# A hybrid decoder layer: nudged half chunks of weights run low x high first, one more half chunk is nudged, and the last query transposes move half a chunk later

## The chip, the cores and the metric

The kernel runs on one core of one Trainium2 chip. The metric is the device time of one execution in microseconds (us); lower is better. The engines are TensorE (PE; its weight loads are PEld), VectorE (DVE), ScalarE (ACT), GpSimd (POOL) and SyncE (SP), which issues most DMAs.

## The reference

One layer for 256 tokens of width 2048, in fp32: an RMS norm, one wide input projection, two token mixers side by side (sparse attention "NSA", and a gated DeltaNet), gated and summed, an output projection, and a gated feed-forward network (FFN) of width 5632.

```python
h = rms_norm(x, norm1_w)
proj = h @ w_in
nsa_q, nsa_kv, nsa_g, dn_qkv, dn_z, dn_a, dn_b, merge_g = split(proj)
o_nsa = nsa_mixer(rope(nsa_q), nsa_kv, nsa_g, ...)
o_dn = gated_deltanet(dn_qkv, dn_z, dn_a, dn_b, ...)   # conv of 4 taps, SiLU, l2 norms,
                                                       # a triangular solve per chunk, a scan
g_nsa, g_dn = split(sigmoid(merge_g))
x = x + (g_nsa * (o_nsa @ w_up_nsa) + g_dn * (o_dn @ w_up_dn)) @ w_o
h2 = rms_norm(x, norm2_w)
x = x + (silu(h2 @ w_ffn_gate) * (h2 @ w_ffn_up)) @ w_ffn_down
out = rms_norm(x, norm_f_w)
```

## The kernel before

**Three matmuls for one.** Every large matrix product is made of fp32r matmuls. Weights and activations are each split into a high part and a remainder, and high x high, high x low and low x high are summed in PSUM; low x low is left out. Activations are kept in this form (`hh`, `odn`, `onsa`, `h2`). Weights come from HBM in chunks of 1 MB (`raw`, three buffers). Each chunk is split in two half chunks by `split`: ScalarE writes the high part (`hi`, line 161), VectorE the remainder (`lo`, line 162), each into one of three buffers.

**group_t**, the function that the change is mostly about, makes two transposed output tiles of 128 features by 256 tokens. The weights are the stationary operand, the activations move. One call takes one or two chunks of 8 blocks of 128 rows, and a half chunk is 24 matmuls on line 238 of 128x256: 16 with the weights `hi` (8 by the activation's high part, 8 by its low part), then 8 with `lo`. In the trace a half chunk is a row `mm<-hh,hi` x16 and a row `mm<-hh,lo` x8; in the text these are the high run and the low run. From about 55 us on, group_t makes the DeltaNet inputs, the NSA inputs, the merge gates, both up projections (`odn`, `onsa`) and the FFN's gate and up products (`h`), which are 88 chunks.

**Work between the half chunks.** After each half chunk `pump` moves one step on in each of three lanes of Python generators; what they emit lands at that place of TensorE's order. `prep_k`, `prep_v`, `prep_q` are run for two groups of four heads each: they convolve (`conv_taps`, line 403 on VectorE, a SiLU on line 407 of ScalarE), transpose on TensorE in plain fp32 (`ktr`, `vtr`, `qtr`), and make products of 128x128 (`G`, `A`). `solve` does the triangular solve on VectorE (lines 497 and 499) and begins with one small transpose `bT`. Each `yield` in a generator is a delay of half a chunk. TensorE follows its order strictly; VectorE's and ScalarE's orders come from a scheduler, which puts the splits well ahead.

**The nudge.** After most of the fp32 pieces the generators set `self.nudge = True`. The next half chunk of group_t then writes its `lo` 16 floats (64 bytes) further into its buffer, and the flag is cleared:

```python
hv, lv = self.split(rv, 256, h, 16 * self.nudge)
self.nudge = False
```

Thirteen half chunks are nudged: behind gcT, both ktr, both G, both vtr, both qtr, both A, at the start of the `odn` products, and behind the transposes R of the second norm's factor, at the start of the FFN. The half chunk behind bT is not.

Of the kernel before, what the change touches and what calls it, by code (L numbers as in the profile page):

```python
# [14 lines left out]
P = 128  # L15
# [82 lines left out]
class Kern:  # L98
# [122 lines left out]
    def group_t(self, srcs, acts, out=None):  # L221

        nc = self.nc
        ps = self.pmain.tile([P, 2, 512], F32, tag="mm", name=self.nm("mm"))[:, :, 0:256]
        n = len(srcs)
        for c, src in enumerate(srcs):
            rv = self.load(src, 256, nk=8)
            for h in range(2):  # L230

                hv, lv = self.split(rv, 256, h, 16 * self.nudge)
                self.nudge = False
                for p in range(3):
                    for k in range(4):
                        a = acts(c * 8 + h * 4 + k)
                        for f in range(2):
                            nc.tensor.matmul(ps[:, f], (hv, hv, lv)[p][:, k, f * P:f * P + P], a[:, p % 2, :],  # L238
                                             start=c + h + p + k == 0, stop=c == n - 1 and h + p + k == 6,
                                             skip_group_check=True)  # L240
                self.pump()
        if out is None:
            return ps
        nc.scalar.activation(out, ps, AF.Copy)
        return out
# [211 lines left out]
    def solve(self):  # L457

        nc, V = self.nc, self.nc.vector
        ar = self.ar  # L460
        Lb = ar.alloc([32, 32], "xm")
        Tb = ar.alloc([32, 32], "xm")
        pr = ar.alloc([32, 32], "xm")
        bank = self.aux("bT")
        self.pin(nc.tensor.transpose(bank[:16, :128], self.brk[:].rearrange("p a b -> p (a b)"), self.cs["ident"]))
        bT = self.ar.alloc([128])
        V.tensor_copy(bT[:16, :], bank[:16, :128])
        bb = self.small([32], "bb")
        for blk in range(4):
            self.pin(nc.gpsimd.dma_start(bb[16 * blk:16 * blk + 16, :], bT[:16, 32 * blk:32 * blk + 32]))  # L470
        bT.free()
        scr = self.dram.tile([4, 16, 32, 32], F32, name="scrM")
        scrT = self.dram.tile([64, 32, 32], F32, name="scrT")
        scrTT = self.dram.tile([64, 32, 32], F32, name="scrTT")
        nc.gpsimd.memset(Tb[:64], 0.0)
        nc.gpsimd.memset(Tb[:64].rearrange("p a b -> p (a b)")[:, 0:1024:33], 1.0)
        for b in range(4):
            sl = slice(32 * b, 32 * b + 32)
            nc.gpsimd.dma_start(scr[b].rearrange("h j i -> j h i"), self.MT[sl, :, sl])
        nc.gpsimd.dma_start(Lb[:64], scr[:].rearrange("b h j i -> (b h) j i"))  # L480
        self.D = ar.alloc([16, 128], "wm")
        self.DT = ar.alloc([16, 128], "wm")
        nc.gpsimd.memset(self.D.ap, 0.0)
        nc.gpsimd.memset(self.DT.ap, 0.0)

        for q in range(4):
            self.pin(V.tensor_tensor(self.MT[:, 4 * q:4 * q + 4, :], self.MT[:, 4 * q:4 * q + 4, :],
                                     self.cs["offmask"][:, None, :].to_broadcast([P, 4, 128]), op=OP.mult))
            if q % 2:
                yield  # L490
        self.pin(V.tensor_tensor(Lb[:64], Lb[:64], bb[:64, None, :].to_broadcast([64, 32, 32]), op=OP.mult))
        yield
        prf = pr[:64].rearrange("p a b -> p (a b)")
        for j in range(31):
            n, m = 31 - j, j + 1
            pv = prf[:, :n * m].rearrange("p (a b) -> p a b", b=m)
            self.pin(V.tensor_tensor(pv, Lb[:64, j, j + 1:32].unsqueeze(2).to_broadcast([64, n, m]),  # L497
                                     Tb[:64, j, 0:m].unsqueeze(1).to_broadcast([64, n, m]), op=OP.mult))
            self.pin(V.tensor_tensor(Tb[:64, j + 1:32, 0:m], Tb[:64, j + 1:32, 0:m], pv, op=OP.subtract))
            if j % 2 or 10 < j < 20:  # L500
                yield
        diag = [slice(32 * b, 32 * b + 32) for b in range(4)]
        nc.gpsimd.dma_start(scrT[:], Tb[:64])
        for b, sl in enumerate(diag):
            nc.gpsimd.dma_start(self.D[sl, :, sl], scrT[16 * b:16 * b + 16].rearrange("h i c -> i h c"))
        for _ in range(2):
            yield
        self.pin(nc.scalar.activation(pr[:64], Tb[:64].rearrange("p a b -> p b a"), AF.Copy))
        nc.gpsimd.dma_start(scrTT[:], pr[:64])
        for b, sl in enumerate(diag):  # L510
            nc.gpsimd.dma_start(self.DT[sl, :, sl], scrTT[16 * b:16 * b + 16].rearrange("h c i -> c h i"))
        Lb.free()
        Tb.free()
        pr.free()
        for _ in range(6):
            yield
# [17 lines left out]
    def prep_q(self, pre, cT, hg):  # L534
        nc, V = self.nc, self.nc.vector
        yield from self.conv_taps(pre, cT, hg * 4)
        yield
        self.qT[hg] = cT
        ss = self.small([2, 4], "ssq", bufs=2)
        for t in range(2):  # L540
            bank = self.aux("qtr")
            bv = self.v4(bank)
            for j in range(4):
                nc.tensor.transpose(bv[:, j, :], cT[:, j, t * P:(t + 1) * P], self.cs["ident"])
            sq = self.ar.alloc([4, 128], "zyxm")
            nc.scalar.activation(sq.ap, bv, AF.Square)
            V.tensor_reduce(ss[:, t, :], sq.ap, axis=AX.X, op=OP.add)
            sq.free()
        self.nudge = True
        V.tensor_scalar(ss[:], ss[:], EPS, None, op0=OP.add)  # L550
        rq = self.rsqrt(ss[:], [2, 4], "rq")
        V.tensor_scalar(self.cq[:, :, hg * 4:hg * 4 + 4], rq[:], SCALE, None, op0=OP.mult)
        for _ in range(3):
            yield
        for t in range(2):
            self.nudge = True
            bank = self.aux("A")
            bv = self.v4(bank)
            for j in range(4):
                nc.tensor.matmul(bv[:, j, :], self.kT[hg][:, j, t * P:(t + 1) * P], cT[:, j, t * P:(t + 1) * P], start=True, stop=True)  # L560
            E = self.E[t, hg]
            V.tensor_tensor(E.ap, bv, E.ap, op=OP.mult)
            self.attnT[t, hg] = E
        for _ in range(2):
            yield
# [1031 lines left out]
```

## Time and profile before

| | |
|---|---|
| median of 3 runs | 1456.73 us (1455.71 to 1456.77) |
| the profiled execution | 1456.47 us, of which 1454.7 us are the span from first to last instruction |
| granted TensorE clock, mean | 0.997 |
| busy share of the span | TensorE 99%, VectorE 67%, ScalarE 49%, GpSimd 9% |

A row of a timeline gives start (us from the span's start), busy us, engine, line, operation, out<-in, shape and count; in brackets stands the idle time before it and what ended it. Equal instructions that follow each other are one row. Matmuls overlap, so the busy time of a row reaches into the next one; how long a run keeps TensorE is the difference of the starts of two rows.

### The profile page before, as it was taken

Reading aid. Unit: us, or ns where it says so; the run is one execution under the profiler, and the core shown is the slowest. Engines: PE = TensorE matmul, PEld = TensorE weight load, DVE = VectorE, ACT = ScalarE, POOL = GpSimd, SP = SyncE. Lnnn points to the kernel's source line nnn. Section 1 sums busy time; section 2 is a strip of 40 time slices with the busy share of each in tenths; the row PEclk is TensorE's granted clock in tenths of the full one; section 3 lists DMA queues with packets and bytes.
Section 4 is the critical chain, followed back from the end, with each engine's and each line's share of the span. In section 5 each row is a group of like instructions: output and inputs, shape, how many; then the busy total and the mean of one; then the engine's idle time right before and its main releaser. Section 6 shows DMA issues by size and latency. Waiting matters only on the chain.

```text
span 1454.7 us, 26218 instructions
## 1 busy us (share of the span) xinstructions
PE 1440.7 (99%) x10985; PEld 1377.0 (95%) x10985; DVE 981.5 (67%) x1425; ACT 710.7 (49%) x880; POOL 128.8 (9%) x93
## 2 busy tenths in 40 slices
PE   9999999999999999999999999999999999999996
PEld 9999999999999999998899999999999998888885
DVE  7678997767687755566565555555555558778776
ACT  6655444355455546445454444444434446545554
POOL 1000101000000000120000000000000002313221
PEclk9999999999999999999999999999999999999998
DMA  8664546345554455555555555555555555555653
GB/s 286 230 213 174 181 164 222 121 145 204 201 200 146 146 203 178 194 195 187 179 198 193 188 200 198 183 200 199 184 197 203 184 193 183 195 206 213 210 195 131
DMA packets 48023, 277.12 MB, mean 191 GB/s; under 512 B 5776, under 2 KB 6304, under 8 KB 22048
## 3 DMA queue, kind: packets, MB, share of 16 engines
q1 hardware_dynamic: 44928, 267.98, 52.7%
q10 hardware_dynamic: 1872, 4.82, 0.9%
q0 software_dynamic: 1104, 2.64, 0.6%
q8 instruction: 86, 1.41, 0.4%
q14 instruction: 33, 0.27, 0.1%
HBM read 272.52 MB, written 2.89 MB: 189 GB/s over the span
## 4 chain that ended last, share of the span: by engine, by line
PE 96%; DVE 3%; DMA 0%; issue 0%; ACT 0%; SPq 0%; DVEq 0%; ACTq 0%
PE mm L238 64%; PE mm L1367 5%; PE mm L1365 5%; PE mm L1366 5%; PE mm L265 4%; PE mm L266 3%; PE mm L264 3%; DVE lo L162 1%; PE oacc L931 1%; PE U L601 1%; PE mmx L1367 1%; PE mmx L1365 1%; PE mmx L1366 1%; DMA raw<-in_zab 0%; DVE main L403 0%; DVE xs L497 0%
## 5 line engine op out<-in xcount | busy, mean ns | idle before, releaser
L162 DVE TENSOR_TENSOR lo<-raw,hi 128x1024 fp32r<-128x1024 f32 (+2 forms) x422 | 508.2, 1206 | 297.8 <-ACT hi L161 296.8
L161 ACT ACTIVATE hi<-raw 128x1024 fp32r<-128x1024 f32 (+2 forms) x422 | 440.3, 1046 | 501.9 <-PE mm L238 382.9
L238 PE MATMUL mm<-h,hi 128*128 128x256 f32 x2816 | 348.5, 276 | 0.0
L238 PEld LDWEIGHTS mm<-h,hi 128*128 128x128 f32 x2816 | 332.6, 188 | 0.1
L238 PE MATMUL mm<-hh,hi 128*128 128x256 f32 x2304 | 291.1, 279 | 0.0
L238 PEld LDWEIGHTS mm<-hh,hi 128*128 128x128 f32 x2304 | 275.3, 188 | 0.6 <-ACT hi L161 0.4
L238 PE MATMUL mm<-h,lo 128*128 128x256 f32 x1408 | 188.2, 276 | 0.0
L238 PEld LDWEIGHTS mm<-h,lo 128*128 128x128 f32 x1408 | 172.7, 188 | 0.0
L238 PE MATMUL mm<-hh,lo 128*128 128x256 f32 x1152 | 155.6, 277 | 0.0
L238 PEld LDWEIGHTS mm<-hh,lo 128*128 128x128 f32 x1152 | 142.6, 188 | 0.0
L1354 DVE TENSOR_TENSOR lo<-raw,hi 128x1024 fp32r<-128x1024 f32 (+1 forms) x88 | 122.4, 1402 | 23.9 <-ACT hi L1353 23.0
L1353 ACT ACTIVATE hi<-raw 128x1024 fp32r<-128x1024 f32 (+1 forms) x88 | 88.1, 1001 | 73.0 <-PE mm L1367 47.7
L1260 POOL TENSOR_TENSOR sgt<-sgt,R 128x512 f32<-128x512 f32 x22 | 33.3, 1513 | 530.1 <-ACT sgt L1259 530.1
L265 PE MATMUL mm<-lo,xa 128*128 128x512 f32 x128 | 50.1, 392 | 0.0
L266 PE MATMUL mm<-hi,xa 128*128 128x512 f32 x128 | 50.1, 391 | 0.0
L264 PE MATMUL mm<-hi,xa 128*128 128x512 f32 x128 | 49.8, 389 | 0.0
L1181 POOL TENSOR_TENSOR main<-main 128x512 f32<-128x512 f32 x7 | 15.1, 2163 | 379.2 <-DVE main L1180 379.2
L265 PE MATMUL mm<-lo,hh 128*128 128x354 f32 (+2 forms) x128 | 44.2, 346 | 0.4 <-DVE lo L150 0.3
L264 PE MATMUL mm<-hi,hh 128*128 128x354 f32 (+2 forms) x128 | 43.9, 349 | 0.3 <-ACT hi L148 0.2
L266 PE MATMUL mm<-hi,hh 128*128 128x354 f32 (+2 forms) x128 | 43.7, 341 | 0.0
L1366 PE MATMUL mm<-lo,fa 128*128 128x512 f32 x112 | 43.7, 390 | 0.0
L1353 ACT ACTIVATE hi<-d 128x1024 fp32r<-128x1024 f32 x24 | 25.5, 1061 | 37.3 <-PE mm L1367 20.0
(400 smaller groups left out, 1766.8 us busy)
## 6 DMA issues: line engine op xcount, KB each, us to landing
raw<-in_wfg SPq DMA_DIRECT2D x88, 1024.0 KB, 4.7
raw<-in_wd SPq DMA_DIRECT2D x88, 512.0 KB, 4.2
raw<-in_wmg SPq DMA_DIRECT2D x32, 1024.0 KB, 4.8
raw<-in_wdn SPq DMA_DIRECT2D x24, 1024.0 KB, 4.8
raw<-in_nsa SPq DMA_DIRECT2D x16, 1024.0 KB, 4.7
raw<-in_wo SPq DMA_DIRECT2D x16, 1024.0 KB, 4.8
raw<-in_wud SPq DMA_DIRECT2D x8, 1024.0 KB, 4.8
raw<-in_wun SPq DMA_DIRECT2D x8, 1024.0 KB, 4.8
```

Of the source, the lines that this page charges most:

```text
L161: nc.scalar.activation(hv, rv[:, m * h:m * h + m, :], AF.Copy)
L162: nc.vector.tensor_tensor(lv, rv[:, m * h:m * h + m, :], hv.bitcast(F32), op=OP.subtract)
L238: nc.tensor.matmul(ps[:, f], (hv, hv, lv)[p][:, k, f * P:f * P + P], a[:, p % 2, :], start=c + h + p + k == 0, stop=c == n - 1 and h + p + ...
L264: nc.tensor.matmul(o, a[:, 0, sl], hv[:, k, :], start=begin, stop=False)
L265: nc.tensor.matmul(o, a[:, 0, sl], lv[:, k, :], start=False, stop=False)
L266: nc.tensor.matmul(o, a[:, 1, sl], hv[:, k, :], start=False, stop=last)
L1260: nc.gpsimd.tensor_tensor(sgt[:], sgt[:], self.R2b, op=OP.mult)
L1353: nc.scalar.activation(hv, v, AF.Copy)
L1354: V.tensor_tensor(lv, v, hv.bitcast(F32), op=OP.subtract)
L1365: nc.tensor.matmul(bank, ahi, hv[:, k, :], start=begin, stop=False)
L1366: nc.tensor.matmul(bank, ahi, lv[:, k, :], start=False, stop=False)
L1367: nc.tensor.matmul(bank, alo, hv[:, k, :], start=False, stop=last)
```

## The change

In group_t the twelve pairs of (part, block) of a half chunk are now listed ahead. A nudged half chunk takes part 2 first (`lo` by the activation's high part), then parts 0 and 1 (`hi` by high, `hi` by low); others keep 0, 1, 2. The flags of the first and the last matmul of a sum follow the place in the list. `solve` sets the nudge behind bT, so there are fourteen nudged half chunks. `prep_q` yields twice instead of once for the second group of query heads.

```diff
@@ group_t
                 hv, lv = self.split(rv, 256, h, 16 * self.nudge)
+                runs = [(p, k) for p in ((2, 0, 1) if self.nudge else (0, 1, 2)) for k in range(4)]
                 self.nudge = False
-                for p in range(3):
-                    for k in range(4):
-                        a = acts(c * 8 + h * 4 + k)
-                        for f in range(2):
-                            nc.tensor.matmul(ps[:, f], (hv, hv, lv)[p][:, k, f * P:f * P + P], a[:, p % 2, :],
-                                             start=c + h + p + k == 0, stop=c == n - 1 and h + p + k == 6,
-                                             skip_group_check=True)
+                for r, (p, k) in enumerate(runs):
+                    a = acts(c * 8 + h * 4 + k)
+                    for f in range(2):
+                        nc.tensor.matmul(ps[:, f], (hv, hv, lv)[p][:, k, f * P:f * P + P], a[:, p % 2, :],
+                                         start=c + h + r == 0, stop=c == n - 1 and h == 1 and r == 11,
+                                         skip_group_check=True)
@@ solve
         self.pin(nc.tensor.transpose(bank[:16, :128], self.brk[:].rearrange("p a b -> p (a b)"), self.cs["ident"]))
+        self.nudge = True
@@ prep_q
         yield from self.conv_taps(pre, cT, hg * 4)
-        yield
+        for _ in range(1 + hg):
+            yield
```

TensorE's order around bT, before (`hi_1904` and `lo_1905` are one half chunk, nudged behind G; `hi_1959` and `lo_1960` the next):

```order
L451 MATMUL G_1897<-main 128x128 x4
L238 MATMUL mm_1786<-hh,hi_1904 128x256 x16
L238 MATMUL mm_1786<-hh,lo_1905 128x256 x8
L465 MATMUL bT_1932<-consts,brk_715 16x128
L238 MATMUL mm_1956<-hh,hi_1959 128x256 x16
L238 MATMUL mm_1956<-hh,lo_1960 128x256 x8
L238 MATMUL mm_1956<-hh,hi_1989 128x256 x16
```

The same place now:

```order
L451 MATMUL G_1897<-main 128x128 x4
L238 MATMUL mm_1786<-hh,lo_1905 128x256 x8
L238 MATMUL mm_1786<-hh,hi_1904 128x256 x16
L465 MATMUL bT_1932<-consts,brk_715 16x128
L238 MATMUL mm_1956<-hh,lo_1960 128x256 x8
L238 MATMUL mm_1956<-hh,hi_1959 128x256 x16
L238 MATMUL mm_1956<-hh,hi_1989 128x256 x16
```

Both half chunks now start with their low run; the third, not nudged, still starts with its high run.

TensorE's order from the last query transposes to the half chunk behind the second A, before:

```order
L238 MATMUL mm_2560<-hh,lo_2663 128x256 x8
L544 MATMUL qtr_2695<-consts,main 128x128 x4
L544 MATMUL qtr_2702<-consts,main 128x128 x4
L238 MATMUL mm_2724<-hh,hi_2727 128x256 x16
L238 MATMUL mm_2724<-hh,lo_2728 128x256 x8
L238 MATMUL mm_2724<-hh,hi_2759 128x256 x16
L238 MATMUL mm_2724<-hh,lo_2760 128x256 x8
L238 MATMUL mm_2724<-hh,hi_2796 128x256 x16
L238 MATMUL mm_2724<-hh,lo_2797 128x256 x8
L560 MATMUL A_2824<-main 128x128 x4
L560 MATMUL A_2830<-main 128x128 x4
L238 MATMUL mm_2724<-hh,hi_2836 128x256 x16
```

And now:

```order
L238 MATMUL mm_2695<-hh,lo_2699 128x256 x8
L546 MATMUL qtr_2731<-consts,main 128x128 x4
L546 MATMUL qtr_2738<-consts,main 128x128 x4
L238 MATMUL mm_2695<-hh,lo_2760 128x256 x8
L238 MATMUL mm_2695<-hh,hi_2759 128x256 x16
L238 MATMUL mm_2695<-hh,hi_2796 128x256 x16
L238 MATMUL mm_2695<-hh,lo_2797 128x256 x8
L238 MATMUL mm_2695<-hh,hi_2824 128x256 x16
L238 MATMUL mm_2695<-hh,lo_2825 128x256 x8
L562 MATMUL A_2858<-main 128x128 x4
L562 MATMUL A_2864<-main 128x128 x4
L238 MATMUL mm_2871<-hh,lo_2875 128x256 x8
```

The transposes and A each stand one half chunk later (`hi_2698` and `lo_2699`, the first half chunk of its group, now precede the transposes), and the nudged half chunk behind A is now the first of the next group, `lo_2875`.

VectorE's order up to the remainder `lo_2875`, before (`xs` on lines 497 and 499 are steps of the solve, `ssq` and `rq` belong to the queries' norm, `ys` and `zkh` to the NSA keys):

```order
L497 TENSOR_TENSOR xs<-xs 64x87
L281 TENSOR_TENSOR rq_u_2711<-rq_y_2710 128x8
L752 TENSOR_SCALAR zkh<-ones 128x4
L499 TENSOR_TENSOR xs<-xs 64x3x29
L282 SCALAR_TENSOR_TENSOR rq_u_2711<-rq_u_2711,ssq_2694 128x8
L728 TENSOR_TENSOR ys<-ys,consts 64x512
L162 TENSOR_TENSOR lo_2875<-raw_2872,hi_2874 128x1024
```

And now:

```order
L549 TENSOR_REDUCE ssq_2730<-zsg 128x4
L498 TENSOR_TENSOR xs<-xs 64x60
L552 TENSOR_SCALAR ssq_2730<-ssq_2730 128x8
L754 TENSOR_SCALAR zkh<-ones 128x4
L500 TENSOR_TENSOR xs<-xs 64x2x30
L279 TENSOR_SCALAR rq_y_2746<-ssq_2730 128x8
L753 TENSOR_TENSOR zkh<-smalls,zkh 128x32
L498 TENSOR_TENSOR xs<-xs 64x31
L281 TENSOR_TENSOR rq_u_2747<-rq_y_2746 128x8
L733 TENSOR_TENSOR ys<-ys,consts 128x512
L162 TENSOR_TENSOR lo_2875<-raw_2872,hi_2874 128x1024
```

Ahead of `lo_2875` now stand, more than before, three steps of the solve and two operations on `ys`, and two small ones fewer; the queries' reduces come later. Other stretches of VectorE's order are changed in the same way.

## The prediction

> **What bounds the kernel now.** I read the page first: shares of the span, then the chain that ended last, then the costliest groups.
>
> ```profile
> span 1454.7 us, 26218 instructions
> PE 96%; DVE 3%; DMA 0%; issue 0%; ACT 0%; SPq 0%; DVEq 0%; ACTq 0%
> L238 PE MATMUL mm<-h,hi 128*128 128x256 f32 x2816 | 348.5, 276 | 0.0
> ```
>
> TensorE is 96% of the chain: time is won or lost only where its matmuls stand closer together or where it waits. The mean of 276 ns is a latency, since matmuls overlap; their pace is the distance between starts. So the second view is TensorE's timeline (start, busy us, line, count), first around the solve's transpose bT.
>
> ```profile
> 157.73 2.13 PE L238 MATMUL mm<-hh,hi 128*128 128x256 f32 x16
> 159.70 1.11 PE L238 MATMUL mm<-hh,lo 128*128 128x256 f32 x8
> 160.65 0.27 PE L465 MATMUL bT<-consts,brk 128*16 128x128 f32 x1
> 160.67 2.13 PE L238 MATMUL mm<-hh,hi 128*128 128x256 f32 x16
> 162.64 1.10 PE L238 MATMUL mm<-hh,lo 128*128 128x256 f32 x8
> 163.58 2.05 PE L238 MATMUL mm<-hh,hi 128*128 128x256 f32 x16
> 165.47 1.10 PE L238 MATMUL mm<-hh,lo 128*128 128x256 f32 x8
> 166.41 2.05 PE L238 MATMUL mm<-hh,hi 128*128 128x256 f32 x16
> 168.29 1.11 PE L238 MATMUL mm<-hh,lo 128*128 128x256 f32 x8
> 169.24 1.03 PE L527 MATMUL vtr<-consts,ys 128*128 128x128 f32 x8
> 170.03 2.13 PE L238 MATMUL mm<-hh,hi 128*128 128x256 f32 x16
> 172.00 1.11 PE L238 MATMUL mm<-hh,lo 128*128 128x256 f32 x8
> 172.95 1.99 PE L238 MATMUL mm<-hh,hi 128*128 128x256 f32 x16
> 174.78 1.07 PE L238 MATMUL mm<-hh,lo 128*128 128x256 f32 x8
> ```
>
> Take differences of starts. The same 16 high matmuls need 1.89 us at 163.58 and 166.41 (118 ns each), but 1.83 at 172.95. There are two paces. After fp32 pieces (vtr, bT) the stream comes in slow: 1.97 us, that is one first gap of 0.20 and fifteen of 0.118. It stays slow for three half chunks after bT, which has no nudge; after vtr, whose half chunk is nudged, the low run still takes 0.95, and the next high run is nearly at the fast pace. What the fast pace is, the next view tells, around the last query transposes; here the wait is seen too.
>
> ```profile
> 218.45 1.07 PE L238 MATMUL mm<-hh,lo 128*128 128x256 f32 x8
> 220.13 1.09 PE L544 MATMUL qtr<-consts,main 128*128 128x128 f32 x8 [0.61 <-ACT main L407]
> 220.98 2.13 PE L238 MATMUL mm<-hh,hi 128*128 128x256 f32 x16
> 226.63 1.98 PE L238 MATMUL mm<-hh,hi 128*128 128x256 f32 x16
> 228.45 1.07 PE L238 MATMUL mm<-hh,lo 128*128 128x256 f32 x8
> 229.35 1.95 PE L560 MATMUL A<-main 128*128 128x128 f32 x16
> 231.06 2.13 PE L238 MATMUL mm<-hh,hi 128*128 128x256 f32 x16
> ```
>
> A fast half chunk is 229.35 - 226.63 = 2.72 us (1.82 + 0.90), a slow one 166.41 - 163.58 = 2.83: 0.11 apart. The low run at 218.45 would end its slot at 219.35; the transposes start at 220.13, so 0.78 us are lost to the SiLU (L407) that makes their input, and they then take 0.85 instead of vtr's 0.79.
>
> **The nudged halves: low first.** Thirteen halves are nudged before the change. Nine enter slow; 157.73 is one, and the last, behind R's transposes, stands at 743.35. Three enter less slowly, like 119.31. One, at 553.72, has no fp32 piece ahead of it.
>
> ```profile
> 743.35 2.13 PE L238 MATMUL mm<-h,hi 128*128 128x256 f32 x16
> 745.32 1.11 PE L238 MATMUL mm<-h,lo 128*128 128x256 f32 x8
> 119.31 2.08 PE L238 MATMUL mm<-hh,hi 128*128 128x256 f32 x16
> 121.22 1.10 PE L238 MATMUL mm<-hh,lo 128*128 128x256 f32 x8
> 122.17 1.99 PE L238 MATMUL mm<-hh,hi 128*128 128x256 f32 x16
> 553.72 2.06 PE L238 MATMUL mm<-odn,hi 128*128 128x256 f32 x16
> 555.62 1.11 PE L238 MATMUL mm<-odn,lo 128*128 128x256 f32 x8
> 556.57 1.99 PE L238 MATMUL mm<-odn,hi 128*128 128x256 f32 x16
> ```
>
> Today a slow entry costs 1.97 + 0.95 - 2.72 = 0.20 over a fast half, and 0.01 to 0.02 in the next (1.83 for 1.82): 0.22. With the low run first, I put the same pieces in the new order: first gap 0.20, seven nudged low matmuls at 0.95/8 = 0.119, so 1.03; then the high run as the one at 172.95, 1.83. That is 2.86, or 0.14 over, and saves 0.08. Nine times: 0.72. At 119.31 today costs 1.91 + 0.95 - 2.72 + 0.01 = 0.15: saved 0.01 to 0.04 each, three times about 0.08. At 553.72 (1.90 + 0.95) no first gap: it keeps 0.045 + 0.01 and saves 0.08. Sum 0.88 us. Nothing hides it, since TensorE is the chain. The ends: no trace shows a nudged low run straight after fp32 pieces. At best it is fast at once, leaving the first gap alone (0.09 over): 0.05 more on each of 13, 0.65. At worst it does not change the pace at all; that is a rival below. The nearest row is the low run cut by fp32 pieces at 469.39, at plain addresses:
>
> ```profile
> 469.39 0.67 PE L931 MATMUL oacc<-main 128*128 128x128 f32 x4
> 469.81 0.72 PE L238 MATMUL mm<-hh,lo 128*128 128x256 f32 x4
> 470.37 1.98 PE L238 MATMUL mm<-hh,hi 128*128 128x256 f32 x16
> 472.18 1.07 PE L238 MATMUL mm<-hh,lo 128*128 128x256 f32 x8
> ```
>
> Its four low matmuls enter slowly (0.56 = 0.20 + three of 0.12) and the high run behind is fast, 1.81. So coming in low first does not spoil the way out, and I take the middle value.
>
> The high weights of a nudged half now come free 0.95 us later. What waits for that is ScalarE's split for the third half after it, which begins 2 x 2.72 us after the nudged one ends; that cover hides it, and without it each of the 14 would cost up to 0.95.
>
> **One more nudge behind bT.** The three halves from 160.67 to 169.24 take 8.57, against 3 x 2.72 = 8.16: 0.41 over. Entered low first they keep 0.14: 0.27 saved.
>
> **The last queries half a chunk later.** Moved are eight transposes, two squares on ScalarE, two reduces and the root's small operations on VectorE, the sixteen A matmuls and their two products; no DMA of this step. The P matmuls, which `dn_main` emits once the A matmuls are out, keep their place in TensorE's order, so nothing behind A is late. Other work of VectorE's list changes places too: the solve's steps go ahead of the queries' root, so its DMAs on GpSimd's queue leave no later. TensorE runs one more weight half first, 219.35 to 222.07, when the SiLU (ready at 220.13) is two us old: the 0.78 goes, and 0.06 of the slow first transposes.
>
> A wait can come in its place. A nudged half that starts low first needs VectorE's remainder at its first matmul, not 1.82 us later. VectorE's timeline shows no idle time from 174 to 236 us; four of its rows, the first the remainder for the half behind the transposes, the second `lo_2875`:
>
> ```profile
> 221.24 1.21 DVE L162 TENSOR_TENSOR lo<-raw,hi 128x1024 fp32r<-128x1024 f32 x1
> 230.40 1.23 DVE L162 TENSOR_TENSOR lo<-raw,hi 128x1024 fp32r<-128x1024 f32 x1
> 231.94 0.69 DVE L729 TENSOR_TENSOR ys<-ys,consts 64x512 f32<-64x512 f32 x1
> 232.95 0.68 DVE L731 TENSOR_TENSOR ys<-ys,consts 128x512 f32<-128x512 f32 x1
> ```
>
> After the transposes the remainder is the one that ended at 222.45, with the same operations ahead of it as before; TensorE asks at 222.07 + 0.79 = 222.86, and earlier savings bring that nearer by some 0.2 more than VectorE (which follows TensorE until vtr at 169.24, then runs without pause): a lead of 0.2, no wait. After A the remainder is lo_2875, which ended at 231.63 and is now behind five more operations, the two rows at 231.94 and 232.95 (0.69 + 0.68) and three small ones, and ahead of two small ones: some 1.4 later, 233.0. TensorE gets there at 222.86 + 2.86 + 2 x 2.72 + 1.70 (A) = 232.86, less 0.3 for savings that VectorE doesn't share: it waits about 0.4. Queued behind it is all of TensorE, so it counts in full. Ends: 0, if VectorE also runs earlier, and 1.0, if it shares none of the savings. Between them 0.4 is nearest to the rows. Net: 0.84 - 0.4 = 0.44.
>
> **Sum.** 0.88 + 0.27 + 0.44 = 1.6 us. The profiled execution took 1456.47 (its span and 1.8 around it) and would take 1454.9; the median of the runs is 0.26 higher, so 1455.1, or 0.11% less. A measurement of this kernel can hardly tell 0.2% (2.9 us) from no change, so this counts as the same.
>
> **The rivals.**
> *Fails to bring the pace back* (slower). If eight nudged matmuls straight after fp32 pieces don't leave the high run fast, the stream stays slow until something else disturbs it. Little matters up front, but after R's transposes (743.35) come the FFN's h matmuls: 2816/16 = 176 halves, about 171 of them after R with no fp32 piece between, each 0.11 slower: +18.8, less the 1.6: 1474. Against it: all 11 nudged halves of the trace with a plain half next left a high run of 1.83, from slow entry, from fast entry and from none alike; and 470.37. For it: each came from a high run. It decides by the high run after a nudged low run: 1.83 or 1.89. 0.08. The milder form, failing only in front of 553.72's 32 halves (wud and wun), costs 3.5: 1458.6, chance 0.04.
> *Order does nothing.* The slow pace might pass only after 24 matmuls, so that a half low first costs 0.22 as now; then only bT (0.41 - 0.22 = 0.19) and the queries remain, 0.6: 1456.1, and with the wait after A at 1.0 it is 1456.7. Or neither order nor address of weights has a price, the pace passing by itself; then the queries' 0.44 alone remain: 1456.3. For both: today the pace changes only in the half after. Against the second: the three halves after bT don't pass by themselves. Chance 0.12 together.
> The Trainium skill's TensorE: Matmul & The Clock Gate, under Step-by-step: what each phase is for, says that weights and moving operand have separate read ports, so that loading the next weights takes nothing from the running matmul. By that rule the second form would hold. The trace disagrees so far: equal matmuls run at 118 and at 113 ns, and the low run 64 bytes higher at 119.
> *More than forecast*, fast at once and no wait: 1.6 + 0.65 + 0.4 = 2.65, 1454.1; past 2.9 us only if transposes gain too. 0.06, half of it past the bound.
>
> **How the numbers follow.** Forecast 0.70, rivals 0.08, 0.04, 0.12, 0.06. Likeliest 1455.1. The range of 8 in 10 goes from the best ends (1454.1, less 0.3 for the spread of runs) to order doing nothing with the long wait and the spread (1456.7 + 0.7): 1453.8 to 1457.4; it leaves out the failures. Faster by over 0.2%: 0.03. Slower: 0.08 and a part of the milder form, 0.09. Same: 0.88.
>
> **What would show it.** Nudged halves: low run of 8 at 1.03, then a high run at 1.83, and the next at 1.81. After bT: three halves in 8.3 instead of 8.57. Query transposes without idle time ahead; a wait for lo L162 of about 0.4 ahead of the low run after A. High runs after R at 1.81. Wrong it would be by 1.89 in these, or by a low run that waits in more places than this one.

## The result and the profile after

The changed kernel takes 1477.02 us, the median of 13 runs, against 1456.49 for the kernel before on the same chip, also 13 runs: a ratio of 1.0132 with a 95% interval of 1.0117 to 1.0147. Forecast were 1455.1 us and a range of 1453.8 to 1457.4. What happened is the rival "Fails to bring the pace back", which had 1474 us and a chance of 0.08.

The page of the kernel after, its span and the group of the FFN's high matmuls:

```profile
span 1475.2 us, 26215 instructions
L238 PE MATMUL mm<-h,hi 128*128 128x256 f32 x2816 | 360.5, 281 | 0.0
```

The mean latency of the same 2816 matmuls went from 276 to 281 ns. The distance between their starts is in the timeline of TensorE. First before the change, from the nudged low run behind R on (its start, 743.35, is shown in the prediction), with the last low run of the FFN's first part:

```profile
746.27 2.00 PE L238 MATMUL mm<-h,hi 128*128 128x256 f32 x16
748.11 1.07 PE L238 MATMUL mm<-h,lo 128*128 128x256 f32 x8
...
1210.50 1.07 PE L238 MATMUL mm<-h,lo 128*128 128x256 f32 x8
```

The same place after the change:

```profile
745.92 1.19 PE L238 MATMUL mm<-h,lo 128*128 128x256 f32 x8
746.95 3.93 PE L238 MATMUL mm<-h,hi 128*128 128x256 f32 x32
750.72 1.10 PE L238 MATMUL mm<-h,lo 128*128 128x256 f32 x8
...
1231.25 1.10 PE L238 MATMUL mm<-h,lo 128*128 128x256 f32 x8
```

Two high runs now follow each other, hence x32. They take 750.72 - 746.95 = 3.77 us, 118 ns each, where 3.63 would be the fast pace. And it stays so: from the first to the last low run shown are 170 half chunks in both kernels, (1231.25 - 750.72)/170 = 2.827 us each after, (1210.50 - 748.11)/170 = 2.720 before. The difference, 0.1067 us, times 171 is 18.2.

It isn't the clock. One window of the FFN in each kernel, before and then after (length, then busy time and instructions of PE, PEld, DVE, ACT and POOL, then the granted clock, the DMA share and GB/s):

```profile
750.00:1210.00 460.00, 460.00 (x4061) 460.00 (x4060) 246.31 (x235) 203.33 (x207) 31.98 (x21) 1.00 0.56 194
```

```profile
750.00:1231.00 481.00, 481.00 (x4086) 481.00 (x4085) 247.90 (x236) 204.26 (x209) 32.16 (x22) 1.00 0.53 186
```

The granted clock is 1.00 in both.

Split at the same events, the 20.5 us of the two spans lie here:

| stage | before | after | difference |
|---|---|---|---|
| start to the half behind gcT | 61.22 | 61.74 | +0.52 |
| to the first `odn` half | 492.50 | 494.62 | +2.12 |
| to the half behind R | 189.63 | 189.56 | -0.07 |
| to the end | 711.35 | 729.28 | +17.93 |

No half chunk of the first stage is nudged, and in the twelve traces of this case it took from 61.09 to 62.88 us, so its 0.52 says nothing of the change.

Around bT the change did what it says. The timeline of TensorE after:

```profile
163.49 1.20 PE L238 MATMUL mm<-hh,lo 128*128 128x256 f32 x8
164.52 3.81 PE L238 MATMUL mm<-hh,hi 128*128 128x256 f32 x32
168.16 1.07 PE L238 MATMUL mm<-hh,lo 128*128 128x256 f32 x8
...
171.79 1.03 PE L528 MATMUL vtr<-consts,ys 128*128 128x128 f32 x8
```

The low run takes 1.03, the 32 high matmuls 3.64, and the three halves 171.79 - 163.49 = 8.30 us instead of 8.57. So the same edit gave the fast pace here and not behind R. Around the last queries it looks like this; the brackets hold the idle time before a row and what ended it:

```profile
225.27 1.04 PE L546 MATMUL qtr<-consts,main 128*128 128x128 f32 x8
226.57 1.21 PE L238 MATMUL mm<-hh,lo 128*128 128x256 f32 x8 [0.26 <-DVE lo L162]
...
235.16 1.95 PE L562 MATMUL A<-main 128*128 128x128 f32 x16
237.59 1.21 PE L238 MATMUL mm<-hh,lo 128*128 128x256 f32 x8 [0.48 <-DVE lo L162]
```

The wait for the SiLU ahead of the transposes is gone, and two waits for VectorE's remainder have come. By starts, the first is 226.57 - (225.27 + 0.79) = 0.51 us, the second 237.59 - (235.16 + 1.70) = 0.73.

### The profile page after: what moved, and what is told of

It reads as the page before. It is cut to its first block, busy times and chain, and to the rows that moved or that the text cites. A ratio compares the mean times of both kernels' runs of the same rounds, so it can differ in the third digit from the quotient of the medians.

```text
span 1475.2 us, 26215 instructions
## 1 busy us (share of the span) xinstructions
PE 1461.2 (99%) x10985; PEld 1397.5 (95%) x10985; DVE 982.0 (67%) x1425; ACT 709.7 (48%) x880; POOL 127.6 (9%) x93
## 4 chain that ended last, share of the span: by engine, by line
PE 83%; DVE 4%; issue 0%; DMA 0%; DVEq 0%
PE mm L238 55%; PE mm L1369 5%; PE mm L1367 5%; PE mm L1368 5%; PE mm L266 2%; PE mm L265 2%; PE mm L264 2%; DVE lo L162 1%; PE oacc L933 1%; PE U L603 1%; PE mmx L1369 1%; PE mmx L1367 1%; PE mmx L1368 1%; DVE xs L500 1%; DVE xs L498 1%
## 5 line engine op out<-in xcount | busy, mean ns | idle before, releaser
L238 PE MATMUL mm<-h,hi 128*128 128x256 f32 x2816 | 360.5, 281 | 0.0
L238 PEld LDWEIGHTS mm<-h,hi 128*128 128x128 f32 x2816 | 344.6, 189 | 0.1
L238 PE MATMUL mm<-h,lo 128*128 128x256 f32 x1408 | 194.4, 281 | 0.0
L238 PEld LDWEIGHTS mm<-h,lo 128*128 128x128 f32 x1408 | 178.0, 189 | 0.0
L1369 PE MATMUL mm<-hi,fa 128*128 128x512 f32 x112 | 43.6, 389 | 0.0
```

Of the source, the lines that this page charges most:

```text
L1369: nc.tensor.matmul(bank, alo, hv[:, k, :], start=False, stop=last)
```

## Single gaps: what tells the two outcomes apart

Of the fourteen nudged halves of the changed kernel seven leave the stream fast (behind the first G, the second ktr, bT, the second vtr, the first qtr, the second A, and at `odn`), seven leave it slow (behind gcT, the first ktr, the first vtr, the second G, the first A, the second qtr, and R). The rows of the timeline sum over eight matmuls; the trace also has each start by itself. The distances between the starts, in ns, through a nudged low run and into the next run:

```
after, R           201 118 122 120 119 115 117 118 | 117 119 117 118 118 117 118   slow
after, gcT         221 119 121 120 120 115 117 118 | 117 118 118 117 119 117 118   slow
after, second ktr  200 119 121 119 121 119 121 117 | 118 122 116 114 113 114 113   fast
after, bT          204 116 119 121 120 119 115 118 | 117 123 118 114 113 113 114   fast
before, R          120 118 118 122 120 119 115 117 | 118 122 119 113 113 114 113   fast
```

Inside a nudged run the gaps go through a cycle of about five, 122 120 119 115 117. Where the run stops in this cycle goes together with what comes behind. When the 115 stands sixth of eight, so that the run ends on 115, 117, 118, the next run goes on at 118. When it stands third or seventh, or there is none (the cycle is cut at 120, 119, 117 or 121, 117), the next run passes through 118, 122, 119 or the like and then goes at 113. This reading is first stated in the expectation of the run with six nudged, after four experiments; the traces of the later ones did not shape it.

## Experiments

**High first again.** The changed kernel with the old order of the parts; bT's nudge and the later queries stay.

```diff
-runs = [(p, k) for p in ((2, 0, 1) if self.nudge else (0, 1, 2)) for k in range(4)]
+runs = [(p, k) for p in (0, 1, 2) for k in range(4)]
```

> The changed kernel with nudged halves high first again; the nudge behind bT and the later query transposes stay. Theory A (phase): eight nudged matmuls shift the stream's timing; begun from the settled pace of a high run they always leave the fast pace behind, begun straight after fp32 pieces they start elsewhere and the end is luck. Theory B (place): the pace changes only where a nudged low run ends a half chunk and the next half chunk's weights, in another buffer, follow. Theory C: order has no part in it, the pace after R is luck. A and B: all 14 nudged halves are followed by high runs of 1.83, time 1456.5 - 0.2 (bT) - 0.8 (queries) = 1455.5. C: high runs after R at 1.89 again, about 1475.

Measured: 1455.51 us against 1456.15, ratio 0.9996 [0.9986, 1.0006]. TensorE's timeline behind R, and around bT:

```profile
744.32 1.11 PE L238 MATMUL mm<-h,lo 128*128 128x256 f32 x8
745.26 1.99 PE L238 MATMUL mm<-h,hi 128*128 128x256 f32 x16
747.10 1.07 PE L238 MATMUL mm<-h,lo 128*128 128x256 f32 x8
```

```profile
162.63 1.10 PE L238 MATMUL mm<-hh,lo 128*128 128x256 f32 x8
163.58 2.05 PE L238 MATMUL mm<-hh,hi 128*128 128x256 f32 x16
165.46 1.11 PE L238 MATMUL mm<-hh,lo 128*128 128x256 f32 x8
```

The time is the one expected, but not for the reason given there, since two of the fourteen places failed. The loss came with the order of the parts, not with the other two edits: behind R the high run takes 747.10 - 745.26 = 1.84 again. But high first is no safe order either. bT's half is nudged here and still leaves a high run of 1.88, and so does the second vtr's. Both low runs have the gaps 113 116 124 120 119 115 117 118: a 115 in sixth place.

**High first at R alone.**

```diff
-runs = [(p, k) for p in ((2, 0, 1) if self.nudge else (0, 1, 2)) for k in range(4)]
+runs = [(p, k) for p in ((2, 0, 1) if self.nudge and not self.late else (0, 1, 2)) for k in range(4)]
...
+            self.nudge = self.late = True    # ahead of R
```

> The changed kernel with the single nudged half behind R (the FFN's first transposes) high first, the other 13 low first. A and B: the FFN's 171 halves are back at 2.72, 1477.0 - 171 x 0.113 = 1457.7, and up to R everything as in the changed kernel. C: about 1477 as before the edit, or fast by luck only.

Measured: 1458.79 us in one run. The timeline behind R:

```profile
747.37 1.11 PE L238 MATMUL mm<-h,lo 128*128 128x256 f32 x8
748.32 1.99 PE L238 MATMUL mm<-h,hi 128*128 128x256 f32 x16
750.15 1.07 PE L238 MATMUL mm<-h,lo 128*128 128x256 f32 x8
```

One half chunk of 24 matmuls, put in the other order, is worth 1477.02 - 1458.79 = 18.2 us. That is the 171 halves.

**Low in the middle.** Parts in the order 0, 2, 1: `hi` by high, `lo`, `hi` by low.

```diff
-(2, 0, 1) if self.nudge
+(0, 2, 1) if self.nudge
```

> The changed kernel with nudged halves in the order high x high, low x high, high x low: 8 high, 8 nudged low, 8 high. A: the nudged run again starts from a high run at its settled pace, so all 14 leave a fast pace, now within the half: 0.20 + 7 x 0.118 + 0.95 + 0.92 = 2.90 instead of 2.92, time about 1455.0. B: the nudged run doesn't end the half, so many fail as with low first, at R too: 1475 or more.

Measured: 1474.96 us, ratio 1.0133 [1.0118, 1.0148]. Behind R:

```profile
744.63 1.10 PE L238 MATMUL mm<-h,lo 128*128 128x256 f32 x8
745.57 2.99 PE L238 MATMUL mm<-h,hi 128*128 128x256 f32 x24
748.40 1.10 PE L238 MATMUL mm<-h,lo 128*128 128x256 f32 x8
```

Slow: 2.83 for 24 high matmuls, gaps in the low run 112 117 123 120 119 115 118 117. Five of the fourteen places stay slow (both G, bT, the first A, R), nine get fast. The time is near the second theory's 1475, but nine fast places speak against that theory too. Eight high matmuls ahead of the low run do not save it, so it is not the place straight behind fp32 pieces that is at fault; and a low run need not be the last of its half to work.

**Low first at plain addresses.**

```diff
-hv, lv = self.split(rv, 256, h, 16 * self.nudge)
+hv, lv = self.split(rv, 256, h, 0)
```

> The changed kernel with nudged halves low first but no shift of 64 bytes: order alone. A and B: nothing changes the pace, so every slow entry stays slow until the next fp32 piece, behind odn and R too: against the changed kernel some 55 more slow halves x 0.113, about 1483. C: no different from the changed kernel, 1477.

Measured: 1477.5 us in one run. The high runs behind gcT and behind R:

```profile
62.13 3.79 PE L238 MATMUL mm<-hh,hi 128*128 128x256 f32 x32
65.75 1.07 PE L238 MATMUL mm<-hh,lo 128*128 128x256 f32 x8
...
747.41 3.93 PE L238 MATMUL mm<-h,hi 128*128 128x256 f32 x32
751.18 1.11 PE L238 MATMUL mm<-h,lo 128*128 128x256 f32 x8
```

The total is close to that of the changed kernel. R has the same share in both, but the rest comes from other places (492.40 us instead of 494.62 from gcT to `odn`, 192.89 instead of 189.56 from there to R): the half behind gcT is fast here (3.62 for its 32 high matmuls) and slow there, bT's the other way round. Behind R they take 3.77, and the gaps of the low run are 200 119 117 118 118 118 117 118, no cycle, the plain slow pace. Where the stream comes in slow at plain addresses it stays slow; where it is fast, as behind gcT, the fp32 pieces themselves let it in fast. So within a stream it is the shift that changes a slow pace, when anything does, and the equal total is no proof that it does nothing.

**Twice the shift.**

```diff
-hv, lv = self.split(rv, 256, h, 16 * self.nudge)
+hv, lv = self.split(rv, 256, h, 32 * self.nudge)
```

> The changed kernel with the low weights of nudged halves 128 bytes higher instead of 64. If 128 bytes are as good as none: low runs at a steady pace and a time as with no shift, 1477.5. If any shift will do: gaps as with 64 bytes, 1477. Neither theory says which.

Measured: 1459.46 us in one run. Behind R:

```profile
747.77 3.79 PE L238 MATMUL mm<-h,hi 128*128 128x256 f32 x32
751.40 1.07 PE L238 MATMUL mm<-h,lo 128*128 128x256 f32 x8
```

128 bytes bring the fast pace behind R too (3.63), but leave gcT, the second qtr and the second A slow. The gaps in R's low run are 202 117 118 117 119 117 118 116, nothing like the cycle of 64 bytes. The distance matters, not only whether there is one. Why these runs come out fast was not found.

**Six nudged instead of eight, and a control.** If the place in the cycle decides, a nudged run two matmuls shorter ends before 115, 117, 118. Block 3 of the low weights is stored at the plain address, the other three 64 bytes higher; since VectorE then writes the remainder in two operations, the control has two operations too, with all four blocks shifted. The sums are the same. Of the edit, the two operations, in a new function for the nudged halves:

```diff
+            nc.vector.tensor_tensor(l0, rv[:, 4 * h:4 * h + 3, :], hv[:, 0:3, :].bitcast(F32), op=OP.subtract)
+            nc.vector.tensor_tensor(l3, rv[:, 4 * h + 3, :], hv[:, 3, :].bitcast(F32), op=OP.subtract)
```

And the one line in which the two runs differ, from the control to six:

```diff
-        l3 = lo[:, 16:16 + 256]     # control: eight nudged
+        l3 = lo[:, 0:0 + 256]       # six nudged
```

> The changed kernel, but of a nudged half's eight low matmuls the last two (block 3) read weights at the plain address: six nudged, two plain, then the high run. Theory A in the form that the traces so far give: at nudged addresses the gaps go round in a cycle of about five (122, 120, 119, 115, 117), and a stretch that is left just after the 115 or later in the cycle by two steps falls to the slow pace, otherwise to the fast. Behind R the 115 is the sixth of eight gaps and the pace stays slow; with six nudged matmuls the stretch ends ahead of it, so the FFN should be fast: 1477.0 - 171 x 0.113 = 1457.7, and gcT, the first ktr, the second G, the first A and the second qtr should turn fast as well, 34 halves or 3.8 more: about 1454 to 1458, since the seven places that are fast now may turn slow. Theory B (the pace changes only where a nudged run ends its half): the FFN stays slow, 1477.

> The control: the same two operations of VectorE and the same order of blocks in the buffer as with six nudged, but all eight low matmuls at addresses 64 bytes higher. A and B: as the changed kernel, the FFN slow, about 1477.

Measured: 1456.62 us with six, 1477.72 with eight, one run each. Behind R with six:

```profile
744.30 3.79 PE L254 MATMUL mm<-h,hi 128*128 128x256 f32 x32
747.93 1.07 PE L254 MATMUL mm<-h,lo 128*128 128x256 f32 x8
```

With eight:

```profile
747.22 3.93 PE L254 MATMUL mm<-h,hi 128*128 128x256 f32 x32
750.99 1.10 PE L254 MATMUL mm<-h,lo 128*128 128x256 f32 x8
```

3.63 against 3.77. With six, every one of the fourteen places leaves the stream fast; with eight, nine stay slow. The gaps behind R:

```
six    201 119 121 120 119 117 123 117 | 114 114 113 113 113 114 114
eight  201 118 122 120 119 115 118 117 | 118 118 117 118 118 118 117
```

They enter alike and part at the sixth gap, where the address of the coming weights differs. 21 us hang on the address of one block of 256 columns in fourteen halves. No run nudged any other number of matmuls than six or eight, so that the place in the cycle decides, and not the number itself, rests on the sorting of the traces further down.

**Six at R alone,** the rest as in the changed kernel.

> The changed kernel, with six nudged and two plain low matmuls at R's half chunk alone (block 3 stored at the plain address by a second VectorE operation; the sums are the same). Phase theory: the 32 high matmuls behind R take 3.63 us, 171 halves are 0.113 faster, 1458.5, while the halves behind gcT, the first ktr and vtr, the second G, the first A and the second qtr stay slow. Rival (low first straight after fp32 pieces can't bring the fast pace, and the run with six at all places differed elsewhere): 1477.

Measured: 1460.04 us in one run (the kernel before on that chip: 1455.92).

```profile
748.12 3.79 PE L252 MATMUL mm<-h,hi 128*128 128x256 f32 x32
751.74 1.07 PE L252 MATMUL mm<-h,lo 128*128 128x256 f32 x8
```

Fast, 3.62 for the 32. The time is 1.5 us more than expected, and 1.14 of them lie ahead of the first nudged half (62.88 us instead of 61.74 up to the half behind gcT), where the two programs are alike; from there to `odn` the stage took 494.65 us against 494.62.

**The queries alone.** The kernel before, with only the later transposes.

```diff
 yield from self.conv_taps(pre, cT, hg * 4)
-yield
+for _ in range(1 + hg):
+    yield
```

> The kernel before with only the query transposes half a chunk later: nudged halves high first, none behind bT. A and B: nothing else changes, the wait of 0.78 and the slow first transposes go: 1456.2 - 0.8 = 1455.4, no wait for lo behind the transposes or A, three slow halves behind bT as before, the half behind the second vtr fast again.

Measured: 1456.38 us against 1456.15, ratio 1.0001 [0.9992, 1.001].

```profile
223.61 2.13 PE L238 MATMUL mm<-hh,hi 128*128 128x256 f32 x16
225.58 1.10 PE L238 MATMUL mm<-hh,lo 128*128 128x256 f32 x8
226.52 2.05 PE L238 MATMUL mm<-hh,hi 128*128 128x256 f32 x16
228.40 1.11 PE L238 MATMUL mm<-hh,lo 128*128 128x256 f32 x8
```

No wait is left at this place, and the stage from gcT to `odn` is 491.71 us instead of 492.50, 0.79 less. But the half behind the transposes now stays slow (228.40 - 226.52 = 1.88; a 115 in sixth place), and in the profiled execution the start up to gcT was 0.73 longer, whose cause isn't known. A gain of 0.05% can't be told from none here.

**Six nudged, queries where they were.** Six low first is free of slow places; the waits for VectorE, which the changed kernel has with later queries and low runs in front, might go with the queries put back.

```diff
-for _ in range(1 + hg):
-    yield
+yield
```

> The run of six nudged matmuls at all fourteen places, but the last query transposes where they stood before the change. Phase theory (the nudged run must not end on the slow part of its cycle; six always do not): every half behind fp32 pieces leaves the next ones at 2.72 us, the high run behind R takes 3.63 for 32. If the 1.07 us that TensorE waited ahead of bT with six nudged comes back and the 0.78 ahead of the transposes too: 1456.6. If the wait ahead of bT belonged to the later queries: 1455.3. Rival (six worked at R by chance): 1470 or more.

Measured: 1460.18 us against 1455.92, ratio 1.0027 [1.0016, 1.0039]: slower than the kernel before, and than six nudged with the later queries (1456.62). All places are fast, R with 32 high matmuls in 3.62. The waits of TensorE between 55 and 560 us (engine, line, what for; total, times, longest):

```profile
PE qtr L561 <- ACT main L423: 2.8, 1, 2.8
PE bT L481 <- DVE main L451: 1.0, 1, 1.0
```

And the timeline there:

```profile
222.89 1.33 PE L561 MATMUL qtr<-consts,main 128*128 128x128 f32 x8 [2.76 <-ACT main L423]
223.87 2.06 PE L254 MATMUL mm<-hh,lo 128*128 128x256 f32 x8
225.73 4.42 PE L254 MATMUL mm<-hh,hi 128*128 128x256 f32 x32
229.98 1.07 PE L254 MATMUL mm<-hh,lo 128*128 128x256 f32 x8
```

Windows of the idle time and of the low run behind it, with the columns as above:

```profile
220.13:222.89 2.76, 0.00 (x1) 0.00 (x1) 2.66 (x7) 1.11 (x2) 0.00 (x0) 1.00 0.80 329
223.90:227.00 3.10, 3.10 (x16) 3.10 (x15) 3.03 (x6) 1.80 (x3) 0.00 (x0) 0.50 0.23 53
```

The SiLU waits for the convolution on VectorE and comes 2.8 us late, where it was 0.6 late in the kernel before. The granted clock is still 1.00 during that idle time and falls behind it: in the trace's record of the clock it is 0.50 from 223.60 to 227.01 us, and the matmuls stand 213 ns apart until then. The low run takes 1.86 instead of 1.03, the 32 high ones 4.25 instead of 3.63, the transposes 0.98 instead of 0.79: 1.6 us on top of the wait. No version here beats the kernel before by more than a measurement can tell.

## Why the prediction was wrong, and where it was right

**The step that failed** is "coming in low first does not spoil the way out ... I take the middle value". The row it rested on, the plain low run behind the fp32 piece of 469.39, showed the end of one disturbance only, and a low run at plain addresses is not a nudged one: low first without a shift leaves R slow as well. What the runs showed in its place: a nudged low run put first left the stream slow at seven of the fourteen places, at R with 3.77 us for 32 high matmuls instead of 3.63, and R's half alone, put back to high first, gave 18.2 of the 20.5 us back. The same goes for the argument against the rival, that all 11 nudged halves of the trace left a high run of 1.83. In single gaps all 11 have no 115 in sixth place. They were fast each time because high first came in at other points of the cycle, not because nudging is safe; with the same high-first order the places at bT and the second vtr failed in one experiment, the second qtr in another. Eleven of eleven was taken for a law and was one side of a coin that the change tossed again, fourteen times, with 171 half chunks on one of the throws.

**How well the cycle accounts for it.** In the traces of before, after and six experiments, 103 nudged runs of eight, 64 bytes higher, lead into further matmuls of the kind. In 36 the 115 (a 114 in three of them) stands sixth: all 36 stay slow. In 67 it doesn't: all 67 get fast. Of the 103, 38 come from traces taken after the reading was on record (16 slow, 22 fast). Six nudged, an intervention and not a sorting, cut the runs ahead of that point, and no place stays slow. That the end of the run in the cycle goes with the outcome is shown; why there are two paces, a cycle, and a change between them is not.

**The rival's size.** It said "each 0.11 slower: +18.8, less the 1.6". Measured are 0.107 a half and 17.93 from R to the end. Most of the rest of the difference to 1474 lies between gcT and `odn`, where the rival counted on about 1.4 of the 1.6 and 2.11 were lost (2.12 by the rounded starts). The distances between starts split that: +1.75 between group_t's own matmuls (3357 distances, 388.02 us before and 389.77 after), since six of the other thirteen places failed too; +1.22 from fp32 pieces to the matmul behind them, the two waits; -0.78 ahead of fp32 pieces, the wait that went; -0.08 inside the pieces.

**The rule on read ports.** The Trainium skill's TensorE: Matmul & The Clock Gate, under Step-by-step: what each phase is for, holds that weights and moving operand have separate read ports, so that loading the next weights takes nothing from the running matmul. By the rule, the prediction said, the second form of "Order does nothing" would hold, with 1456.3, and the trace disagreed so far. The runs go on disagreeing with that form: the address of one block of weights makes 1456.62 or 1477.72 us. Whether the read ports are the cause, no run here shows.

**bT** was right: 8.30 for three halves, as the forecast of 0.27 less than 8.57 said. It is one of the seven where the cycle ended well.

**Each low run at 1.03** was right (746.95 - 745.92), and where the stream gets fast the next high run takes 1.82 of the 3.64 for two. So the 0.08 saved at each place is real where the pace comes back, and that was half of them.

**The queries.** The 0.78 went, as said; alone, their move gave 0.79 in its stage. The wait after A is 0.73 instead of 0.4, nearer to the end that the prediction gave for a VectorE that shares no saving (1.0). The wait after the transposes, held to have "a lead of 0.2, no wait", is 0.51. The net of this step is 0.84 - 0.51 - 0.73 = -0.40 instead of +0.44; the lead of VectorE's remainder, which the prediction worked out to 0.2, was the mis-sized term. The prediction had VectorE run "without pause" behind the second vtr, as it does before the change. VectorE's timeline at the solve's first operation on `xs` and `bb`, before and then after:

```profile
178.42 1.21 DVE L491 TENSOR_TENSOR xs<-xs,bb 64x1024 f32<-64x1024 f32 x1
```

```profile
181.10 1.22 DVE L492 TENSOR_TENSOR xs<-xs,bb 64x1024 f32<-64x1024 f32 x1 [1.95 <-DMA xs<-scrM]
```

Now VectorE stands idle for 1.95 us there, and the remainder ends 54.73 us behind the start of vtr (226.52 - 171.79) instead of 53.21 (222.45 - 169.24): 1.5 later. TensorE asks for it 0.65 later than forecast, counted in the same way (226.06 - 171.79 against 222.86 - 169.24). The three traces with high first everywhere (before, the first experiment, the queries alone) have no such idle time, the nine others have 0.38 to 1.95 us of it; how the order of the parts leads to it stays open. With high first (the first experiment and the queries alone) no wait for a remainder is in the trace from 55 to 560 us, nor with low in the middle, so these two belong to low first. They don't always come with it: the control with eight nudged, low first too, has neither.

**One run of 13** of the changed kernel took 1459.29 us, the others 1475.78 to 1477.7. That lies where R's half at the fast pace would put it; it wasn't profiled, so this is only argued. If so, the same program can come out either way at R, and the experiments with one run each could have met such a case. Against chance speak all nine runs with six nudged at R (1456.62, 1460.04, and seven from 1458.75 to 1460.56 us) and all ten with high first everywhere (1454.78 to 1455.82): none has the 18 us.

## What to carry to other kernels

A stream of equal matmuls can have more than one steady pace, and what disturbs it (an fp32 piece, a run at another address) chooses between them; a trick that brings back the fast pace in every place of one trace may do so by where it happens to end, so look at the single gaps, not at sums over a run, before moving it. Price such a place by what runs behind it undisturbed: one half chunk at the FFN's door carried 18 us, and the other thirteen about 2. A low or late operand moved to the front of a group also needs its producer a run earlier, which is a wait as soon as that producer has no idle time.

## What the runs showed of the hardware

- Two paces of the same fp32r matmuls of 128x256, 113 and 118 ns from start to start, each stable for 170 half chunks in a row (2.720 and 2.827 us), at a granted clock of 1.00 in both.
- Weights 64 bytes higher give a cycle of about 122, 120, 119, 115, 117 ns, and the pace behind goes with where it is cut (36 of 36 slow with the 115 sixth, 67 of 67 fast without); 128 bytes give another pattern (117 to 119).
- A difference of 1 ns at the entry goes with it: behind fp32 pieces a first gap of 200 comes with the pattern 119 121 119 121 119 121 117 and a fast way out (three places of the changed kernel's trace), one of 201 or 205 at ktr, vtr, G, A and R with a 115 in the sixth place and a slow one (five). It isn't a rule: with six at R alone, the half behind the second G enters with 200, has its 115 sixth and stays slow.
- After one wait of 2.76 us the granted clock was 0.50 for 3.41 us, from 0.71 us behind the end of the wait on, and the matmuls stood 213 ns apart; waits of up to 1.1 us between 55 and 560 us had no such sequel.
